# One step of a hybrid decoder layer on one core: h goes into the gate unnormalised, half of its tiles turned by transposing DMAs, and the embedding tiles are loaded later

## The chip, the cores and the metric

The kernel runs on one core of one Trainium2 chip. The metric is the device time of one execution in microseconds (us). The engines are called as the profile calls them: PE is TensorE (matrix products), PEld its weight loads, DVE is VectorE, ACT is ScalarE, POOL is GpSimd, and SP is SyncE, which issues most DMAs. All data is float32; products of float32 accuracy are made from two parts of each operand, a high part in the format fp32r and the low remainder (names that end in h and l).

## What is computed

The layer has a part A (gated mixing), a part B (pooling), an output projection, and last a gated embedding. Only the end of the layer matters here:

```
h = h + _rmsnorm(jnp.einsum('bld,de->ble', m, w_out), post_g)
e = jnp.einsum('blp,pd->bld', p, w_ple)
gate = jax.nn.sigmoid(jnp.einsum('bld,de->ble', _rmsnorm(h, ple_in_g), w_pg))
h = h + _rmsnorm(gate * e, ple_out_g)
```

There are 1024 prompt tokens in eight tiles of 128 (tiles 0 to 7) and 8 sample tokens (tile S); the model is 1024 wide. _rmsnorm(h, g) is h times one root per token times the gain g per column.

## The kernel before

**Products.** Each 1024 x 1024 product is done with Strassen's scheme: seven products of half blocks (P1 to P7) instead of eight, on sums of quarters of both operands. The stored operand has parts B11, B21, B22 and the sums T1 to T4, each loaded and cut into a high and a low part; for wg (the gate's weights w_pg) the parts T4 and B22 lie in DRAM already cut (wgcut, tiles wgT4h, wgT4l, wgB22h, wgB22l). The sums are built in the middle of the kernel by column_sums (line 1340): it loads two row blocks of w_pg (wgraw), cuts parts of them, adds and subtracts them in place on VectorE, and stores the results (wglow, wghigh). column_steps (line 1358) hangs this on steps of part B.

**Stages.** The last stages are the output projection (names wo, m, mw) and the gate (wg, h, hw). Both go over four pairs of token tiles: pair i holds tiles 2i and 2i + 1. In both the tokens are the stationary operand, and each pair's sums of quarters (hs) are cut into hw. A product's result (acct, in PSUM) is taken out by ScalarE or VectorE.

**Between the two stages.** After pair i of the output stage, each of its tiles goes through four functions, hung on the steps of the next pair:
- out_finish (line 1408) scales the row, adds x by an accumulating DMA on POOL's queue, and stores h to DRAM by SP.
- gate_norm (line 1417) takes the mean square of h on ScalarE (hn<-h, whose full output is only scratch), the root on VectorE and POOL (ms, rstd), and scales h into hn on VectorE.
- gate_input (line 1425) turns hn into big, eight blocks of 128 x 128, on TensorE (pht<-ident,hn); ScalarE takes each block out with the gain ple_in_g of its row of w_pg as scale (big<-pht,gvec).
- For the sample, gate_input multiplies the gain in sample_stationary (line 801), which writes sst.

**The embedding.** ge_start (line 1453) allocates the gate's output tile ge and loads the stored embedding e into eback. It is called by Embed.loads (line 1490), that is, with the weights of the pair, FETCH = 6 steps ahead. gated (line 1457) applies the sigmoid, multiplies by eback, takes the mean square and, for tiles 6 and 7 and S, multiplies by the gain row out. gate_finish (line 1471) scales by the root and adds h: for tiles 0 to 5 by an accumulating DMA, for the last two by scalar_tensor_tensor (STT) with a loaded hback, in two halves that are stored apart.

**The order.** All instructions from step 3 on are recorded and then ordered by a planner (class Planner, line 56): TensorE's list is the clock, and every other operation gets a due time from it (late) and is placed on its engine by due time, when the planner takes its operands and a slot of SBUF to be free. So a small change can move instructions of all engines. The helpers record all operations, and the profile therefore shows line 299 for each; groups are told apart by tile names. SP and the queue of each engine run in order.

**The transposing DMA that exists already.** For v, in the first stage, v_planes (line 873) splits the 32-bit words of a tile into two planes of 16 bits (vw<-v, on ScalarE), dma_start_transpose turns them (v<-vw, issued on SP), and v_join (line 882) puts the planes together in big (big<-v, on ScalarE).

Of the kernel before, what the change touches and what calls it, by code (L numbers as in the profile page):

```python
# [8 lines left out]
F32 = mybir.dt.float32  # L9
F32R = mybir.dt.float32r  # L10
BF16 = mybir.dt.bfloat16
U16 = mybir.dt.uint16
AF = mybir.ActivationFunctionType
ALU = mybir.AluOpType

P = 128
D = 1024
NB = D // P
# [3 lines left out]
HALF = 512  # L22
# [283 lines left out]
def hybrid_step(  # L306
# [7 lines left out]
    nc = tc.nc  # L314
# [3 lines left out]
    dram = ctx.enter_context(tc.tile_pool(name="spill", bufs=1, space=bass.MemoryType.DRAM))  # L318
# [6 lines left out]
    w_in, w_pa, w_pb, w_out, w_ple, w_pg = w_in[0], w_pa[0], w_pb[0], w_out[0], w_ple[0], w_pg[0]  # L325
# [4 lines left out]
    def slot(name, shape=(P, T), dt=F32):  # L330
        n_name[0] += 1
        return plan.tile(spool.tile(list(shape), dt, tag="slot", name=f"{name}_{n_name[0]}", bufs=SLOTS,
                                    padded_shape=None), "slot")

    def sm(name):
        n_name[0] += 1
        return small.tile([P, 1], F32, tag="sm", name=f"{name}_{n_name[0]}")
# [17 lines left out]
    def dma(out, in_, by=None):  # L355
        (by or nc.sync).dma_start(out=out, in_=in_)
# [11 lines left out]
    ident = cpool.tile([P, P], F32, tag="ident", name="ident")  # L368
# [6 lines left out]
    nc = plan  # L375
# [3 lines left out]
    big = cpool.tile([P, NB, T], F32, tag="big", name="big")  # L379

    def rstd(parts, n=P):

        t, r = sm("ms"), sm("rstd")
        nc.vector.tensor_scalar(out=t[:n], in0=parts[0][:n], scalar1=EPS,
                                scalar2=parts[1][:n] if len(parts) == 2 else 0.0, op0=ALU.add, op1=ALU.add)
        nc.gpsimd.tensor_tensor(out=r[:n], in0=t[:n], in1=mhalf[:n], op=ALU.pow)
        return r

    def root(part, n=P):

        t, r = sm("ms"), sm("rstd")
        nc.vector.tensor_scalar(out=t[:n], in0=part[:n], scalar1=EPS, scalar2=None, op0=ALU.add)
        nc.gpsimd.tensor_tensor(out=r[:n], in0=t[:n], in1=mhalf[:n], op=ALU.pow)
        return r

    def square_sum(src, n=P, bias=0.0, scratch=None):

        s = sm("ssq")
        out = junk[:n, : src.shape[1]] if scratch is None else scratch[:n]
        nc.scalar.activation(out=out, in_=src, func=AF.Square, scale=D ** -0.5, bias=bias, accum_out=s[:n])  # L400
        return s
# [12 lines left out]
    class Operand:  # L414
# [37 lines left out]
        def at(self, what, k):  # L452
            return [part[:, k % 2, :] for part in self.parts[what, k // 2]]
# [237 lines left out]
    class User:  # L691

        func = AF.Copy
# [5 lines left out]
        def loads(self):  # L699
            pass  # L700
# [100 lines left out]
    def sample_stationary(src, nk, gain=None):  # L801

        st = slot("sst", (P, nk, P), F32R)
        nc.gpsimd.memset(f32(st), 0.0)
        ps = bank("psst").rearrange("p (k t) -> p k t", t=16)
        for k in range(nk):
            nc.tensor.transpose(ps[:, k, :NS], src[:NS, k * P : (k + 1) * P], ident[:NS, :NS])
        got = ps[:, :nk, :NS]
        if gain is not None:
            mul(smix_s, got, gain.unsqueeze(2).to_broadcast([P, NB, NS]))  # L810
            got = smix_s
        split(got, st[:, :, :NS], st[:, :, 32 : 32 + NS])
        return st
# [21 lines left out]
    col = lambda i, k: gvec[:, i * NB + k : i * NB + k + 1]  # L835
# [26 lines left out]
    S = NB  # L862
    rows = lambda t: NS if t == S else P
# [4 lines left out]
    NPAIR = NB // 2  # L868
    vsums = cpool.tile([P, NB + 1, NPAIR], F32, tag="vsums", name="vsums")
# [138 lines left out]
    kept = {}  # L1008
# [4 lines left out]
        kept[key + "high"] = dram.tile([HALF, HALF + w], F32, tag=key + "high", name=key + "high")  # L1013
    wgcut = {what: dram.tile([HALF, D], F32, tag="wg" + what, name="wg" + what) for what in ('T4', 'B22')}
    kept["rowsum"] = dram.tile([NB, P], F32, tag="rowsum", name="rowsum")
    kept["h"] = dram.tile([T, D], F32, tag="h", name="h")
    kept["e"] = dram.tile([T, D], F32, tag="e", name="e")

# [20 lines left out]
    def stored(key, src, width, free=None, split=()):  # L1039
        return Stored(key, src, kept[key + "low"], kept[key + "high"], width, free, split)  # L1040
# [7 lines left out]
    class Gate(User):  # L1048
        func = AF.Sigmoid
# [7 lines left out]
    class U(User):  # L1057
        func = AF.Gelu_apprx_tanh
# [4 lines left out]
    class ZA(User):  # L1063
        func = AF.Silu
# [84 lines left out]
    class ZB(User):  # L1149
        func = AF.Silu  # L1150
# [90 lines left out]
    flat, c = big.rearrange("p b t -> p (b t)"), [T + 4 * w for w in (0, HALF, HALF + WIDE, HALF + 2 * WIDE)]  # L1241
# [20 lines left out]
    c = vsteps[0]  # L1262
# [67 lines left out]
    p, l, c = gbsteps[2], gbsteps[3], pasteps[0]  # L1330
    turn_over(yaop, l, [*l[1:], c[0]])
    p, l, c = pasteps[2], pasteps[3], pbsteps[0]
# [7 lines left out]
    def column_sums(key, src, b):  # L1340

        lo, hi = raw = [slot(f"{key}raw", (P, D)) for _ in range(2)]
        for i, t in enumerate(raw):
            dma(t, src[(4 * i + b) * P : (4 * i + b + 1) * P, :])

        def go():
            cuts = wgcut if key == "wg" else {}
            for what, src in (("B11", lo[:, :HALF]), ("B21", hi[:, :HALF]), ("B22", hi[:, HALF:])):
                if what in cuts:
                    store_parts(cuts[what], b, src)  # L1350
            store_sums(key, b, lo, hi, HALF)
            for what, src in (("T2", lo[:, :HALF]), ("T1", lo[:, HALF:]), ("T4", hi[:, :HALF]), ("T3", hi[:, HALF:])):
                if what in cuts:
                    store_parts(cuts[what], b, src)

        return go

    def column_steps(key, src, steps):
        for b, (l, c) in enumerate(steps):
            held = []  # L1360
            at(l, lambda b=b, held=held: held.append(column_sums(key, src, b)))
            at(c, lambda held=held: held[0]())

    column_steps("wo", w_out, [(uflow[8 + 5 * i], uflow[11 + 5 * i]) for i in range(4)])
    bflow = [s for x, z, _ in bsteps for p in (x, z) for s in p]
    column_steps("wg", w_pg, [(bflow[9 + 7 * i], bflow[12 + 7 * i]) for i in range(4)])

    def sample_product(st, op):

# [6 lines left out]
        return left, right  # L1376

    half = lambda j: slice(j * HALF, (j + 1) * HALF)
    h_of, parts, hn_of, samples = {}, {}, {}, {}

    def start(t, name):
        h_of[t], parts[t] = slot(name, (P, D)), []
# [25 lines left out]
    def out_finish(t):  # L1408
# [5 lines left out]
        nc.gpsimd.dma_start(out=h, in_=x_of(t), accum_op=ALU.add)  # L1414
        dma(kept["h"][t * P : t * P + r, :], h)

    def gate_norm(t):

        r = rows(t)
        h = h_of.pop(t)  # L1420
        hn = hn_of[t] = slot("hn", (P, D))
        rs = rstd([square_sum(h[:r], r, scratch=hn)], r)
        nc.vector.tensor_scalar_mul(hn[:r], h[:r], rs[:r])

    def gate_input(t):

        hn = hn_of.pop(t)
        if t == S:
            samples["h"] = sample_stationary(hn, NB, gvec[:, 2 * NB :])
            return  # L1430
        for k4 in range(0, NB, 4):
            ps = bank("pht")
            for k in range(4):
                nc.tensor.transpose(ps[:, k * P : (k + 1) * P], hn[:, (k4 + k) * P : (k4 + k + 1) * P], ident)
            for k in range(4):
                nc.scalar.activation(out=big[:, k4 + k, t * P : (t + 1) * P], in_=ps[:, k * P : (k + 1) * P],
                                     func=AF.Copy, scale=col(2, k4 + k))

    def merged_sample():
        st = samples["m"] = slot("mst", (P, NB, P), F32R)  # L1440
# [12 lines left out]
    def ge_start(t):  # L1453
        ge[t], e_of[t], parts[t] = slot("ge", (P, D)), slot("eback", (P, D)), []
        dma(e_of[t][: rows(t)], kept["e"][t * P : t * P + rows(t), :])

    def gated(t, c, src):
        r = rows(t)
        g = ge[t][:r, c]
        nc.scalar.activation(out=g, in_=src, func=AF.Sigmoid)  # L1460
        mul(g, e_of[t][:r, c], g)
        parts[t].append(square_sum(g, r))
        if len(parts[t]) > 2:
            a, b = parts[t][:2]
            both = sm("both")
            nc.vector.tensor_scalar(out=both[:r], in0=a[:r], scalar1=b[:r], scalar2=None, op0=ALU.add)
            parts[t][:2] = [both]
        if t >= NB - 2:
            mul(g, g, gains["out"][:r, c])
# [17 lines left out]
            dma(y_of(t)[:, half(j)], g[:r, half(j)])  # L1487

    class Embed(User):
        def loads(self):  # L1490
            for m in range(2):
                ge_start(2 * self.pair + m)

        def direct(self, m, j, ps, c=None):
            gated(2 * self.pair + m, c or half(j), ps)

# [20 lines left out]
    LAST = ("P1", "P6", "P7", "P4", "P5", "P3", "P2")  # L1517

    FIRST = ("P1", "P7", "P6", "P2", "P4", "P5", "P3")
    woop, wgop = stored("wo", w_out, HALF), stored("wg", w_pg, HALF, split=wgcut)  # L1520
    outsteps = [strassen(Turned(i, "m"), woop, Out(i), Tokens, None if i else FIRST) for i in range(NPAIR)]
    gatesteps = [strassen(Turned(i, "h"), wgop, Embed(i), Tokens, LAST if i == NPAIR - 1 else None)
                 for i in range(NPAIR)]
# [5 lines left out]
    l, c = pbsteps[3], outsteps[0]  # L1529
    turn_over(woop, l, [*l[2:], c[0], c[1]], ("B11", "T3", "T2", "B21", "T4", "T1", "B22"))  # L1530
    l, c = outsteps[3], gatesteps[0]
    turn_over(wgop, [s if what not in wgcut else e for what, s, e in zip(PARTS, l, [*l[1:], c[0]])], [*l[2:], c[0], c[1]])

    def gain_row(key, src):
        gains[key] = row_broadcast(src, key)

    at(pbsteps[3][4], lambda: gain_row("post", post_g[0]))
    at(outsteps[3][4], lambda: gain_row("out", ple_out_g[0]))
    at(outsteps[0][1], merged_sample)
    at(outsteps[1][2], out_sample)  # L1540
    at(outsteps[1][4], lambda: out_finish(S))
# [183 lines left out]
```

## Time and profile before

| what | value |
|---|---|
| three runs | 993.88, 996.26, 996.41 us (median 996.26) |
| the profiled execution | 993.25 us |
| its span in the profile | 991.5 us |
| PE busy | 977.7 us |
| DVE busy | 802.9 us |
| ACT busy | 522.8 us |
| POOL busy | 69.6 us |
| last product starts | 983.12 us |
| granted clock of TensorE, mean | 0.997 |

Busy times are those of the engine's instructions without waits. In a timeline row stand start, duration, engine, line, operation, tiles (out<-in), shapes and how many follow one another; in brackets the idle time before it and what ended it. A group's row has the least, median and most duration in ns and the first and last start. A busy PE is not PE at its peak, since products overlap; so the distance between starts is used for it. The span leaves out some 1.7 us that the execution's own time has around it.

### The profile page before, as it was taken

The numbers are of one execution on the slowest core, as the hardware profiler recorded it, in microseconds if no ns is written. First come the engines' busy times: TensorE is split into PE (matmuls) and PEld (weight loads), VectorE is DVE, ScalarE is ACT, GpSimd is POOL, SyncE is SP. The second block draws the span as 40 slices with busy tenths as digits, with TensorE's granted clock in tenths as the row PEclk, the third lists the DMA queues.
The fourth block names the chain that finished last, engine by engine and source line by source line (L and its number), as shares of the span: only waits on it lengthen the run. The fifth ranks groups of instructions, "written<-read, shape, count | busy, mean of one in ns | idle before, by whom it ended". The sixth has DMA issues, their size and how long they took to land. (4 is left out here: it accounts for less than half of the span.)

```text
span 991.5 us, 16004 instructions
## 1 busy us (share of the span) xinstructions
PE 977.7 (99%) x6110; PEld 878.0 (89%) x6110; DVE 802.9 (81%) x1245; ACT 522.8 (53%) x923; POOL 69.6 (7%) x142
## 2 busy tenths in 40 slices
PE   8999999999999999999999999999999999999996
PEld 6899989999998999999999999999999988888885
DVE  5976559787769888888897987697799898779797
ACT  7778887565434433243342333562453365678653
POOL 2000001000000000000000100000000002312111
PEclk9999999999999999999999999999999999999998
DMA  9335573322374354564635076873663553389546
GB/s 336 131 107 113 123 151 128 127 84 76 120 258 146 128 196 141 196 209 155 242 118 192 16 260 214 316 282 126 238 233 131 173 186 85 79 279 360 158 109 191
DMA packets 105515, 171.39 MB, mean 173 GB/s; under 512 B 25375, under 2 KB 65775, under 8 KB 105430
## 3 DMA queue, kind: packets, MB, share of 16 engines
q1 hardware_dynamic: 103070, 162.46, 48.2%
q0 software_dynamic: 2048, 7.37, 4.2%
q8 instruction: 48, 0.79, 0.3%
q10 hardware_dynamic: 320, 0.54, 0.2%
q14 instruction: 29, 0.24, 0.1%
HBM read 114.84 MB, written 51.77 MB: 168 GB/s over the span
## 5 line engine op out<-in xcount | busy, mean ns | idle before, releaser
L299 DVE TENSOR_TENSOR u<-acc,u 128x520 f32<-128x520 f32 (+1 forms) x90 | 62.6, 696 | 36.4 <-PE acc L299 31.9
L299 POOL TENSOR_TENSOR rstd<-ms,mhalf 128x1 f32<-128x1 f32 (+1 forms) x45 | 37.3, 830 | 215.7 <-DVE ms L299 215.7
L299 POOL MEMSET u<- 128x8 f32 x35 | 4.7, 135 | 497.5 <-PE acc L299 270.7
L299 ACT ACTIVATE u<-acc 128x512 f32<-128x512 f32 x39 | 23.2, 595 | 27.5 <-PE acc L299 27.1
L299 ACT ACTIVATE paw<-pas 128x512 fp32r<-128x512 f32 x16 | 10.0, 628 | 30.6 <-DVE pas L299 25.2
L299 ACT ACTIVATE pbw<-pbs 128x512 fp32r<-128x512 f32 x16 | 10.0, 629 | 26.8 <-DVE pbs L299 23.7
L299 DVE TENSOR_TENSOR big<-big 128x1024 f32<-128x1024 f32 (+4 forms) x20 | 23.6, 1217 | 0.0
L299 ACT ACTIVATE big<-pht,gvec 128x128 f32<-128x128 f32 x64 | 18.0, 382 | 8.3 <-PE pht L299 8.3
L299 ACT ACTIVATE big<-mix 128x256 f32<-128x256 f32 x32 | 12.1, 383 | 17.3 <-PE mix L299 16.6
L299 ACT ACTIVATE big<-v 128x1024 uint16<-128x1024 uint16 x16 | 18.5, 1174 | 4.7 <-DMA v<-vw 4.7
L299 PE MATMUL accm<-qh,wpoolw 128*128 128x260 f32 (+1 forms) x96 | 20.9, 319 | 0.0
L299 ACT ACT_TABLE_LOAD x13 | 16.7, 1283 | 6.8 <-PE acc L299 5.8
L299 ACT ACTIVATE gbw<-gbs 128x512 fp32r<-128x512 f32 x16 | 10.0, 625 | 15.6 <-DVE gbs L299 13.7
L299 DVE TENSOR_TENSOR acc<-acc,u 128x512 f32<-128x512 f32 (+1 forms) x16 | 11.2, 699 | 8.7 <-PE acc L299 8.7
L299 ACT ACTIVATE zbw<-zbs 128x512 fp32r<-128x512 f32 x16 | 10.1, 629 | 15.1 <-DVE zbs L299 9.5
L299 ACT ACTIVATE zaw<-zas 128x512 fp32r<-128x512 f32 x16 | 10.0, 630 | 14.6 <-DVE zas L299 9.1
L299 ACT ACTIVATE zbw<-zbraw 128x512 fp32r<-128x512 f32 x12 | 7.5, 626 | 19.2 <-DMA zbraw<-in_w_in_dram 10.5
L299 PEld LDWEIGHTS accm<-qh,wpoolw 128*128 128x128 f32 x96 | 15.6, 188 | 1.9
L299 ACT ACTIVATE uw<-us 128x512 fp32r<-128x512 f32 x16 | 10.0, 626 | 13.6 <-DVE us L299 10.8
L299 DVE TENSOR_TENSOR v<-acc,u 128x520 f32<-128x520 f32 (+1 forms) x9 | 6.3, 697 | 13.4 <-PE acc L299 13.4
L299 ACT ACTIVATE gb<-gb 128x1032 f32<-128x1032 f32 (+1 forms) x8 | 6.8, 854 | 18.7 <-DVE gb L299 18.7
L299 ACT ACTIVATE vw<-v 128x1024 uint16<-128x1024 uint16 x16 | 16.1, 1045 | 0.5 <-DVE v L299 0.5
(688 smaller groups left out, 3626.6 us busy)
## 6 DMA issues: line engine op xcount, KB each, us to landing
ga<-ga SPq DMA_DIRECT2D x16, 516.0 KB
gb<-gb SPq DMA_DIRECT2D x16, 516.0 KB
ya<-za SPq DMA_DIRECT2D x8, 516.0 KB
yb<-zb SPq DMA_DIRECT2D x8, 516.0 KB
x<-in_x_prompt_dram SPq DMA_DIRECT2D x8, 512.0 KB
vraw<-in_w_in_dram SPq DMA_DIRECT2D x8, 512.0 KB
e<-e SPq DMA_DIRECT2D x8, 512.0 KB
garaw<-in_w_in_dram SPq DMA_DIRECT2D x8, 512.0 KB
```

The lines of the kernel that those rows point to most:

```text
L299: getattr(getattr(self.nc, e), method)(*args, **kwargs)
```

## The change

1. **No normalisation ahead of the gate.** gate_norm still takes the mean square and the root, but keeps the root in rin(t), a column of vsums, which is free by then. h goes to the product as it is. gated multiplies by the root: scale=rin(t) in the sigmoid. The scaling of hn on VectorE is gone.
2. **The gain ple_in_g goes into w_pg.** column_sums scales both row blocks by the gain on ScalarE before the sums, and stores their left halves to a new DRAM tile, wgleft (the parts B11 and B21 are loaded from there instead of w_pg). The loads and the sums hang on earlier steps of part B: 7 + 7i and 9 + 7i instead of 9 + 7i and 12 + 7i.
3. **Tiles 0 to 3 are turned by DMA.** gate_norm splits h into two planes of 16 bits (hw<-h, two ScalarE instructions; this hw is another tile than the cut sums of that name) and turns them with a transposing DMA back into h; gate_input joins the planes into big (big<-h, two ScalarE instructions). Tiles 4 to 7 are turned by TensorE as before, with one eviction of 512 columns per four blocks instead of four of 128.
4. **The embedding tiles come later.** ge_start is called at step 5 of the pair before instead of with the weights.

```
-        hn = hn_of[t] = slot("hn", (P, D))
-        rs = rstd([square_sum(h[:r], r, scratch=hn)], r)
-        nc.vector.tensor_scalar_mul(hn[:r], h[:r], rs[:r])
+        nc.scalar.activation(out=spare, in_=src, func=AF.Square, scale=D ** -0.5, accum_out=n[:r])
+        root(n, r, rin(t))
+        if t not in BY_DMA:
+            return
+        words = slot("hw", (P, 2, D), U16)
+        for w in range(2):
+            nc.scalar.activation(out=words[:, w], in_=h.bitcast(U16).rearrange("p (c w) -> p w c", w=2)[:, w],
+                                 func=AF.Copy)
+        h_of[t] = h.bitcast(U16).rearrange("p (k t) -> p k t", t=P)
+        nc.sync.dma_start_transpose(out=h_of[t], in_=words.rearrange("p w c -> p (w c)"))
...
+            if t in BY_DMA:
+                nc.scalar.activation(out=words_of(t)[:, k4].rearrange("p k (t w) -> p k t w", w=2),
+                                     in_=got.rearrange("p (w k) t -> p k t w", w=2)[:, k4], func=AF.Copy)
+                continue
...
-            for k in range(4):
-                nc.scalar.activation(out=big[:, k4 + k, t * P : (t + 1) * P], in_=ps[:, k * P : (k + 1) * P],
-                                     func=AF.Copy, scale=col(2, k4 + k))
+            nc.scalar.activation(out=big[:, k4, t * P : (t + 1) * P], in_=ps.rearrange("p (k t) -> p k t", t=P),
+                                 func=AF.Copy)
...
+            for i, t in enumerate(raw if cuts else ()):
+                nc.scalar.activation(out=t, in_=t, func=AF.Copy, scale=col(2, 4 * i + b))
+                dma(kept["wgleft"][(4 * i + b) * P : (4 * i + b + 1) * P, :], t[:, :HALF])
...
-    column_steps("wg", w_pg, [(bflow[9 + 7 * i], bflow[12 + 7 * i]) for i in range(4)])
+    column_steps("wg", w_pg, [(bflow[7 + 7 * i], bflow[9 + 7 * i]) for i in range(4)])
...
-        nc.scalar.activation(out=g, in_=src, func=AF.Sigmoid)
+        nc.scalar.activation(out=g, in_=src, func=AF.Sigmoid, scale=rin(t))
...
-        def loads(self):
-            for m in range(2):
-                ge_start(2 * self.pair + m)
-
...
+    for i in range(NPAIR):
+        at((gatesteps[i - 1] if i else outsteps[3])[5], lambda i=i: [ge_start(2 * i + m) for m in range(2)])
```

How the instructions move is shown at three places. First TensorE, in the output stage, where pair 1 goes from its step P5 (woT1) to P1 of the next product (woB11); before:

```order
L299 MATMUL acct_1331<-woT1l_1267,mw_1308 128x512
L299 MATMUL acct_1331<-woT1h_1266,mw_1308 128x512
L299 MATMUL pht_1339<-ident,hn_1300 128x128 x4
L299 MATMUL pht_1340<-ident,hn_1300 128x128 x4
L299 MATMUL acct_1344<-woB11h_1221,mw_1322 128x512
```

and now:

```order
L299 MATMUL acct_1330<-woT1h_1267,mw_1307 128x512 x2
L299 MATMUL acct_1330<-woT1l_1268,mw_1307 128x512
L299 MATMUL acct_1330<-woT1h_1267,mw_1307 128x512
L299 MATMUL acct_1338<-woB11h_1222,mw_1321 128x512
L299 MATMUL acct_1338<-woB11l_1223,mw_1321 128x512
```

The eight transposes are gone, and the products follow one another; the same holds at three more places. Second SP, where the weights of the gate's first pair are loaded (wgB from w_pg or wgleft, wgT from the stored sums, h<-h the store of h). Before:

```order
L299 DMA wgB_1257_1386<-in_w_pg_dram 128x2x512
L299 DMA eback_1394<-e 128x1024
L299 DMA eback_1392<-e 128x1024
L299 DMA wgT_1268_1397<-wglow 128x2x512
L299 DMA wgT_1269_1398<-wglow 128x2x512
L299 DMA wgB_1285_1414<-in_w_pg_dram 128x2x512
L299 DMA wgB_1286_1415<-in_w_pg_dram 128x2x512
L299 DMA h<-h_1369 128x1024
L299 DMA wgT_1293_1422<-wghigh 128x2x512
```

and now:

```order
L299 DMA wgB_1244_1374<-wgleft 128x2x512
L299 DMA_TRANSPOSE h_1308<-hw_1351 128x16x128
L299 DMA wgT_1251_1381<-wglow 128x2x512
L299 DMA_TRANSPOSE h_1323<-hw_1348 128x16x128
L299 DMA wgT_1252_1382<-wglow 128x2x512
L299 DMA wgB_1264_1394<-wgleft 128x2x512
L299 DMA wgB_1265_1395<-wgleft 128x2x512
L299 DMA wgT_1272_1402<-wghigh 128x2x512
```

The two loads of eback and the store of h have left this stretch (the first load of eback now stands behind wgT4, and one store of h fewer stands ahead of wgT4's end), and the transposing DMAs of tiles 2 and 3 have come in. Third VectorE, at the very end (ge_1550 and ge_1548 before are ge_1546 and ge_1544 now, tiles 7 and 6). Before:

```order
L299 TENSOR_TENSOR ge_1548<-acct_1582,u_1574 128x512
L299 SCALAR_TENSOR_TENSOR ge_1550<-ge_1550,rstd_1585,hback_1586 128x512
L299 TENSOR_TENSOR ge_1548<-eback_1549,ge_1548 128x512
L299 TENSOR_TENSOR ge_1548<-eback_1549,ge_1548 128x256
L299 SCALAR_TENSOR_TENSOR ge_1550<-ge_1550,rstd_1585,hback_1586 128x512
```

and now:

```order
L299 TENSOR_TENSOR ge_1544<-acct_1562,u_1554 128x512
L299 SCALAR_TENSOR_TENSOR ge_1546<-ge_1546,rstd_1565,hback_1566 128x512 x2
L299 TENSOR_TENSOR ge_1544<-eback_1545,ge_1544 128x512
L299 TENSOR_TENSOR ge_1544<-eback_1545,ge_1544 128x256
L299 TENSOR_SCALAR both_1570<-ssq_1567,ssq_1568 128x1
```

Both halves of tile 7's STT now stand ahead of the products with eback for tile 6.

More of the change, by code (lines that the diff above doesn't have):

```diff
@@ L387, in rstd, with root @@
         return r
-    def root(part, n=P):
-        t, r = sm("ms"), sm("rstd")
+    def root(part, n=P, r=None):
+        t, r = sm("ms"), sm("rstd") if r is None else r
         nc.vector.tensor_scalar(out=t[:n], in0=part[:n], scalar1=EPS, scalar2=None, op0=ALU.add)
@@ L1015, in hybrid_step @@
     kept["rowsum"] = dram.tile([NB, P], F32, tag="rowsum", name="rowsum")
+    kept["wgleft"] = dram.tile([D, HALF], F32, tag="wgleft", name="wgleft")
     kept["h"] = dram.tile([T, D], F32, tag="h", name="h")
@@ L1378, in hybrid_step @@
     half = lambda j: slice(j * HALF, (j + 1) * HALF)
-    h_of, parts, hn_of, samples = {}, {}, {}, {}
+    h_of, parts, samples = {}, {}, {}
     def start(t, name):
@@ L1415, in out_finish, with words_of @@
         dma(kept["h"][t * P : t * P + r, :], h)
+    rin = lambda t: vsums[: rows(t), t, :1]
+    BY_DMA = (0, 1, 2, 3)
+    def words_of(t):
+        return big.bitcast(U16)[:, :, 2 * t * P : 2 * (t + 1) * P]
     def gate_norm(t):
         r = rows(t)
-        h = h_of.pop(t)
-        hn = hn_of[t] = slot("hn", (P, D))
-        rs = rstd([square_sum(h[:r], r, scratch=hn)], r)
-        nc.vector.tensor_scalar_mul(hn[:r], h[:r], rs[:r])
+        h = h_of[t]
+        n, spare = sm("ssq"), slot("hspare", (P, D))[:r] if t == S else big[:, :, t * P : (t + 1) * P]
+        src = h[:r] if t == S else h.rearrange("p (k c) -> p k c", c=P)
+        nc.scalar.activation(out=spare, in_=src, func=AF.Square, scale=D ** -0.5, accum_out=n[:r])
[8 more added lines that the diff above has]
+        nc.sync.dma_start_transpose(out=h_of[t], in_=words.rearrange("p w c -> p (w c)"))
@@ L1425, in gate_input @@
     def gate_input(t):
-        hn = hn_of.pop(t)
+        got = h_of.pop(t)
         if t == S:
-            samples["h"] = sample_stationary(hn, NB, gvec[:, 2 * NB :])
+            samples["h"] = sample_stationary(got, NB)
             return
-        for k4 in range(0, NB, 4):
+        for k4 in (slice(0, 4), slice(4, NB)):
+            if t in BY_DMA:
+                nc.scalar.activation(out=words_of(t)[:, k4].rearrange("p k (t w) -> p k t w", w=2),
+                                     in_=got.rearrange("p (w k) t -> p k t w", w=2)[:, k4], func=AF.Copy)
+                continue
@@ L1432, in gate_input @@
             ps = bank("pht")
             for k in range(4):
-                nc.tensor.transpose(ps[:, k * P : (k + 1) * P], hn[:, (k4 + k) * P : (k4 + k + 1) * P], ident)
-            for k in range(4):
-                nc.scalar.activation(out=big[:, k4 + k, t * P : (t + 1) * P], in_=ps[:, k * P : (k + 1) * P],
-                                     func=AF.Copy, scale=col(2, k4 + k))
+                nc.tensor.transpose(ps[:, k * P : (k + 1) * P], got[:, (k4.start + k) * P : (k4.start + k + 1) * P], ident)
@@ L1519, in hybrid_step @@
     FIRST = ("P1", "P7", "P6", "P2", "P4", "P5", "P3")
-    woop, wgop = stored("wo", w_out, HALF), stored("wg", w_pg, HALF, split=wgcut)
+    woop, wgop = stored("wo", w_out, HALF), stored("wg", kept["wgleft"], HALF, split=wgcut)
     outsteps = [strassen(Turned(i, "m"), woop, Out(i), Tokens, None if i else FIRST) for i in range(NPAIR)]
```

## The prediction

> **What bounds the kernel now.** I read the page first, for the shares of the engines, then the waits of TensorE, then the timeline of TensorE around the removed work. From the page:
>
> ```profile
> PE 977.7 (99%) x6110; PEld 878.0 (89%) x6110; DVE 802.9 (81%) x1245; ACT 522.8 (53%) x923; POOL 69.6 (7%) x142
> ```
>
> The reader is to see PE at 977.7 of 991.5 us. The waits of TensorE are seven rows in all, of which these are the first and the last (total, times, longest):
>
> ```profile
> PE warm L299 <- POOL ident masks.py:199: 1.9, 1, 1.9
> ...
> PE state L299 <- DVE big L299: 0.3, 1, 0.3
> ```
>
> The seven sum to 5.7 us and none lies in the output or gate stage. So TensorE sets the end: whatever is taken from its list comes off the time in full, if nobody else becomes late; and work on another engine costs nothing as long as TensorE finds its operands and its PSUM tiles ready.
>
> **What the change removes.** Half of the pht transposes leave TensorE. This is one tile of them in TensorE's timeline before (start, duration, operation):
>
> ```profile
> 848.19 0.40 PE L299 MATMUL acct<-woT1h,mw 128*128 128x512 f32 x1
> 848.43 1.03 PE L299 MATMUL pht<-ident,hn 128*128 128x128 f32 x8
> 849.22 0.48 PE L299 MATMUL acct<-woB11h,mw 128*128 128x512 f32 x1
> 849.54 0.39 PE L299 MATMUL acct<-woB11l,mw 128*128 128x512 f32 x1
> ```
>
> Durations overlap in the pipeline, so starts count. From the first transpose to the next product is 849.22 − 848.43 = 0.79 us; that product is followed after 0.32 us, where the usual step (848.19 to 848.43) is 0.24. The eight transposes so cost 0.79 + 0.08 ≈ 0.88 us, a quarter of what the summed durations would say. Four tiles: 4 × 0.88 = **−3.5 us**. Tiles 4 to 7 stay on TensorE.
>
> VectorE loses the scaling of hn, and ScalarE changes its evictions. Their groups, from the views of the tiles hn and pht (ns: least, median, most), and from the page the two operations that the DMA path uses, as the kernel already does it for v:
>
> ```profile
> L299 DVE TENSOR_SCALAR hn<-h,rstd x8: 732/748/752, 841.0 to 923.9; 128x1024 f32<-128x1024 f32 x8
> L299 ACT ACTIVATE big<-pht,gvec x64: 347/378/415, 849.1 to 927.3; 128x128 f32<-128x128 f32 x64
> L299 ACT ACTIVATE big<-v 128x1024 uint16<-128x1024 uint16 x16 | 18.5, 1174 | 4.7 <-DMA v<-vw 4.7
> L299 ACT ACTIVATE vw<-v 128x1024 uint16<-128x1024 uint16 x16 | 16.1, 1045 | 0.5 <-DVE v L299 0.5
> ```
>
> VectorE: −8 × 0.748 = −6.0 us, off the path, but it is slack where it is full. ScalarE on a DMA tile: two splits and two joins, 2 × 1.045 + 2 × 1.174 = 4.4 us, for eight evictions, 8 × 0.378 = 3.0 summed: +1.4 us, and up to +2.2 since evictions in a row overlap, four times. On a TensorE tile two evictions of 512 columns, about the 0.6 us of u<-acc (595 ns in the page's groups) each, replace eight: about −1 us, four times. ScalarE is the engine with room, so I take nothing for this:
>
> ```profile
> 843.00:873.00 30.00, 30.00 (x149) 24.60 (x148) 23.60 (x43) 21.36 (x58) 9.03 (x11) 1.00 0.34 84
> 873.00:893.00 20.00, 20.00 (x97) 16.45 (x96) 15.28 (x21) 14.04 (x32) 3.44 (x5) 1.00 1.04 331
> 893.00:913.00 20.00, 20.00 (x93) 16.33 (x92) 18.05 (x26) 15.39 (x36) 5.34 (x5) 1.00 1.05 357
> ```
>
> These windows (span; PE, PEld, DVE, ACT, POOL busy; clock; DMA share; GB/s) show ScalarE busy 70 to 77%. They also show what matters more, the last two columns: the DMA engines are two thirds idle until 873 and **full from 873 to 913**.
>
> **What the transposing DMAs cost.** The v stage has eight; two with their joins, from the queues of SP and ScalarE, and what the DMA engines did from 75 to 85 us (40 slices of 0.25 us):
>
> ```profile
> 75.45 1.99 SPq L299 DMA_TRANSPOSE v<-vw  x1
> 79.08 1.77 SPq L299 DMA_TRANSPOSE v<-vw  x1
> ```
>
> ```profile
> 79.85 1.19 ACT L299 ACTIVATE big<-v 128x1024 uint16<-128x1024 uint16 x1 [1.18 <-DMA v<-vw]
> 83.42 1.19 ACT L299 ACTIVATE big<-v 128x1024 uint16<-128x1024 uint16 x1 [0.78 <-DMA v<-vw]
> ```
>
> ```profile
> DMA  0000000999999999922008999999999699899940
> GB/s 0 0 0 0 0 0 5 184 221 213 202 221 217 218 215 196 193 37 41 0 0 162 217 206 218 214 215 222 216 182 217 159 266 233 299 336 348 315 135 21
> ```
>
> A join waited until 4.4 us after the issue (75.45 to 79.85), and 4.3 the second time. Ten full slices, 2.5 us of all sixteen engines, went into one tile at some 215 GB/s. Tiles 0 and 1 turn near 850 to 860, in idle DMA time: free. For one of tiles 2 and 3 the evictions of pht began here before:
>
> ```profile
> 870.98 2.18 ACT L299 ACTIVATE big<-pht,gvec 128x128 f32<-128x128 f32 x8 [0.20 <-PE pht L299]
> ```
>
> In the new order their splits and transposing DMAs stand some instructions behind that place, near 875 to 880, in the full stage: +5.0 us of DMA work ahead of the gate's weights.
>
> [...] The slices above say 215 GB/s, so I go by 2.5.
>
> **Who is late then.** The last loads that TensorE needs early in the gate are the two halves of wgT4. Their issues on SP, and those eight DMAs later (the order has each issue wait for the eighth before it):
>
> ```profile
> 887.71 0.51 SPq L299 DMA_DIRECT2D wgT4h<-wgT  x1
> ...
> 891.29 0.39 SPq L299 DMA_DIRECT2D wgT4h<-wgT  x1
> 892.60 0.36 SPq L299 DMA_DIRECT2D wgT4l<-wgT  x1
> ...
> 899.07 0.36 SPq L299 DMA_DIRECT2D wgB22h<-wgB  x1
> 900.37 0.36 SPq L299 DMA_DIRECT2D wgB22l<-wgB  x1
> 901.96 1.30 SPq L299 DMA_DIRECT2D eback<-e  x2
> ```
>
> The first wgT4h has landed by 899.1, its wgT4l by 900.4, a store of h by 902.0; in steps of about 1.3 us the second pair follows by 902.9 and 904.2 (an estimate from these rows). TensorE reads the second pair here (the second product of the first row is the first on the second half):
>
> ```profile
> 908.35 0.63 PE L299 MATMUL acct<-wgT4h,hw 128*128 128x512 f32 x2
> 908.81 0.39 PE L299 MATMUL acct<-wgT4l,hw 128*128 128x512 f32 x1
> ```
>
> So before there were 908.81 − 904.2 = 4.6 us to spare. The change takes 3.5 of them by TensorE coming earlier. On the DMA side it adds 5.0 us and takes three 512 KB transfers out from ahead of wgT4's end (two eback loads and one store of h, 1.3 us each by the same steps): net +1.1. To that comes up to 1.4 us in which SP stands before a transposing DMA until ScalarE has split its tile, with the queue empty (nothing is left where eback stood). New landing 905.3 to 906.7, wanted at 905.3: a wait of 0 to 1.4 us. Bounds: if transposes ran at the plain rate, no wait; if both slowed plain loads beside them by as much again, 5 us. I take the nearest rows and the low middle, **+0.5 us**. wgB22 has 3 us more to spare (first read at 915.55) and is covered.
>
> **The tail.** The end runs through VectorE, ScalarE and POOL after the last product:
>
> ```profile
> 982.61 0.74 DVE L299 SCALAR_TENSOR_TENSOR ge<-ge,rstd,hback 128x512 f32<-128x512 f32 x1
> 983.40 1.03 DVE L299 TENSOR_TENSOR ge<-eback,ge 128x512 f32<-128x512 f32 x2
> 985.20 0.42 ACT L299 ACTIVATE junk<-ge 128x256 bf16<-128x256 f32 x1 [0.36 <-issue]
> 986.73 1.42 DVE L299 SCALAR_TENSOR_TENSOR ge<-ge,rstd,hback 128x512 f32<-128x512 f32 x2 [0.44 <-POOL rstd L299]
> ```
>
> In the new order both halves of the first STT stand ahead of the eback products; two such take 1.42 us (row 986.73) where one takes 0.74. The products start 0.65 to 0.7 later, and junk, rstd and the last STT with them: **+0.65 us**. The new scale of the sigmoid is hidden under that STT; its price is between nothing and 0.1 us.
>
> **The early part of the change.** Eight scalings of wgraw on ScalarE, eight stores of wgleft and earlier loads lie between 410 and 530 us. A 128x1024 pass of ScalarE took 1.05 us for vw, above. Two windows of the stretch:
>
> ```profile
> 460.00:480.00 20.00, 20.00 (x130) 18.23 (x130) 19.56 (x32) 9.17 (x15) 0.66 (x3) 1.00 0.42 148
> 500.00:520.00 20.00, 20.00 (x135) 18.40 (x135) 19.90 (x31) 8.73 (x14) 1.78 (x5) 1.00 0.27 93
> ```
>
> That is 8.4 us of ScalarE in 120, where it is busy 46%, and DMA time at a share of 0.27 to 0.42: covered, 0. The uncovered part is VectorE, 98% busy: its in-place sums of wgraw now also wait for the wgleft store to have read the tile, with the adds that free TensorE's PSUM queued behind them. No row shows that wait; it is between 0 (the store was issued long before) and the 4 us of a landing above. I take 0, since the steps also start earlier, and keep the other end as a rival.
>
> **Sum**, against the profiled execution's 993.25 us: −3.5 + 0.5 + 0.65 = −2.35, so 990.9. The median of the runs shown is 996.26, 3.0 above that execution; on it the forecast is **993.9**.
>
> **The rivals.**
> 1. *wgT4 is in time* and the tail costs little: −2.85 to −3.5, about 993.1. For it: the slices count a whole tile at 2.5 us though the loads could fill gaps between its packets. Against it: a share of 1.04 from 873 on. [...]
> 2. *VectorE waits for wgleft* between 410 and 530: one or two waits of 2 to 4 us, less a cover that I put at 1 to 2 us: +1.5 on the forecast, 995.4. For it: 19.90 of 20 us busy. Against: DMA is two thirds idle there.
> 3. *Slower: the transposed tiles land late.* A DMA in the full stage lands 11.4 us after its issue (887.71 to 899.07), and with transposes among those ahead up to 13.8; not 4.4. ScalarE meets the first join of tile 2 some 3.5 us after the issue (the instructions between them in the new order) and stands in order, with wgB11h, wgT2h, the hw pieces and the evictions of acct behind it, for 8 to 10 us. The hw pieces bound it: before, the last was ready 3.1 us ahead of the first gate product:
>
> ```profile
> 888.57 0.62 ACT L299 ACTIVATE hw<-big 128x512 fp32r<-128x512 f32 x1
> ```
>
> ```profile
> L299 PE MATMUL acct<-wgB11h,hw x32: 388/396/477, 892.3 to 963.5; 128*128 128x512 f32 x32
> ```
>
> So TensorE would wait 5 to 7 us, wgT4's wait being hidden in it: −2.85 + 6 = +3.15, 999.4. TensorE waits from a landing of 6.6 us on, and the kernel is slower than before from 9.5 us on. For it: the DMA share. Against it: SP stands before this DMA, so little is queued ahead of it. [...]
> 4. *Nothing gained*: TensorE reaches the gate early and waits there for VectorE, which is 18.05 of 20 us busy from 893 to 913. Against: VectorE loses 6.0 us just there. About 996.3.
>
> **How the numbers follow.** Chances: forecast 0.33, rivals 0.28, 0.17, 0.19, 0.03. The bound of 0.3%, about what a measurement of this kernel can tell from no change, is 3.0 us. Faster by more: 0.21 of the first rival and 0.09 of the forecast, 0.30. Slower by more: 0.13 of the third and 0.06 of the second, whose upper end is two waits of 4 us, 0.19. The rest, 0.51, is within. The three runs before spread over 2.5 us, so the low end is the first rival's −3.5 less 1.6: 991.2. The high end is the third's 999.4.
>
> **What would show it.** Right: four pht rows left for 32 matmuls, TensorE's busy time 3.5 us down, at most one new wait of TensorE, on wgT4, under 1.5 us, and a tail of about 9 us from the last product. Wrong: a ScalarE wait for the DMA of h above 5 us, a VectorE wait between 410 and 530, or several TensorE waits on acct or hw in the gate.

## The result and the profile after

The change made the kernel slower: 1011.8 us median of 6 runs (1009.36 to 1016.78) against 996.25 us of 6 runs of the kernel before, ratio 1.0161 with a 95% interval of 1.0142 to 1.018. The forecast was 993.9 us in a range up to 999.4.

Page of the changed kernel, its span and busy times:

```profile
span 1010.7 us, 15931 instructions
...
PE 983.5 (97%) x6078; PEld 879.9 (87%) x6078; DVE 797.8 (79%) x1235; ACT 536.1 (53%) x891; POOL 67.6 (7%) x142
```

VectorE has lost 5.1 us of work and ScalarE gained 13.3, about as worked out. TensorE is busy 5.8 us longer, though 32 matmuls are gone, and no longer 99% of the span. What it waited for from 850 us on (total, times, longest):

```profile
PE acct L299 <- ACT h L299: 6.0, 1, 6.0
PE acct L299 <- DVE h L299: 2.0, 1, 2.0
PE acct L299 <- DMA wgB22l<-wgB: 1.8, 2, 0.9
PE pht L299 <- ACT big L299: 0.8, 1, 0.8
PE acct L299 <- DMA wgB22h<-wgB: 0.6, 1, 0.6
```

Before, there was none of these. I set each matmul of the changed kernel beside the same one of before and followed the difference of their starts. It is +5.2 us before the first removed transposes, falls by 0.85 to 0.88 at each of the four places (to +1.8 at 879 us: the saving is there in full), and then rises to +18.9 at the last matmul. The 5.2 us ahead of the gate are not of the change: TensorE's list is the same up to there, and most of the loss sits at the start (1.6 us) and near 150 us (about 3.1), in instructions that the change does not touch. From 321 to 849 us the difference stays at 5.2, so the work that the change adds between 410 and 530 us cost nothing that shows here.

So the gate lost 17.1 us. ScalarE's queue first, in the first of these views, then SP's and POOL's:

```profile
882.87 0.62 ACT L299 ACTIVATE hw<-big 128x512 fp32r<-128x512 f32 x1
894.30 1.17 ACT L299 ACTIVATE big<-h 128x1024 uint16<-128x1024 uint16 x1 [10.81 <-DMA h<-hw]
895.38 0.57 ACT L299 ACTIVATE junk<-acct 128x512 bf16<-128x512 f32 x1
895.86 0.19 ACT L299 ACTIVATION_READ_ACCUMULATOR junk<-acct 128x1 f32 x1
895.95 0.58 ACT L299 ACTIVATE h<-acct 128x512 f32<-128x512 f32 x1
```

```profile
876.24 1.26 SPq L299 DMA_DIRECT2D wgB<-wgleft  x2
880.48 4.30 SPq L299 DMA_TRANSPOSE h<-hw  x1
884.88 1.02 SPq L299 DMA_DIRECT2D wgT<-wglow  x1
886.00 11.88 SPq L299 DMA_TRANSPOSE h<-hw  x1
897.97 0.53 SPq L299 DMA_DIRECT2D wgT<-wglow  x1
```

```profile
880.44 0.90 POOL L299 DMA_DIRECT2D h<-in_x_prompt_dram  x1 [2.00 <-PE acct L299]
886.04 0.87 POOL L299 DMA_DIRECT2D h<-in_x_prompt_dram  x1 [3.12 <-DVE h L299]
```

The reader is to see three things. The join of tile 2 stood 10.81 us for a transposing DMA that was issued at 880.48 and landed by 894.30: 13.8 us. The eviction h<-acct, for which TensorE waited 6.0 us, stood behind it. And the issue of the second transposing DMA held SP for 11.88 us, with the gate's weights behind it: the second wgT of the first sum was issued only at 897.97. POOL issued an accumulating load of x at the very time of each transpose, and these loads came late too. From the DMA view, the two loads before (issued at 876.65 and 881.50) and now (the last column: us from issue to landing):

```profile
h<-in_x_prompt_dram POOLq DMA_DIRECT2D x1, 512.0 KB, 8.4
h<-in_x_prompt_dram POOLq DMA_DIRECT2D x1, 512.0 KB, 8.6
```

```profile
h<-in_x_prompt_dram POOLq DMA_DIRECT2D x1, 512.0 KB, 13.1
h<-in_x_prompt_dram POOLq DMA_DIRECT2D x1, 512.0 KB, 18.8
```

So the collision has three victims in this trace: ScalarE's joins, SP's list, and the accumulating loads themselves. What the DMA engines and TensorE's clock did meanwhile (some of the windows; the last three columns: clock, DMA share, GB/s):

```profile
879.00:882.00 3.00, 3.00 (x15) 2.45 (x14) 1.96 (x3) 3.00 (x6) 0.90 (x1) 1.00 0.90 314
882.00:885.00 3.00, 3.00 (x15) 2.43 (x14) 2.91 (x4) 1.49 (x3) 0.56 (x1) 1.00 1.28 113
888.00:891.00 3.00, 2.62 (x12) 1.77 (x10) 0.56 (x1) 0.00 (x0) 0.00 (x0) 1.00 1.06 79
891.00:894.00 3.00, 0.00 (x0) 0.00 (x0) 0.00 (x0) 0.00 (x0) 0.00 (x0) 1.00 1.27 109
894.00:906.00 12.00, 9.41 (x34) 7.56 (x35) 5.00 (x7) 6.72 (x11) 0.93 (x1) 0.72 1.23 146
897.00:900.00 3.00, 3.00 (x8) 2.32 (x8) 2.39 (x4) 3.00 (x6) 0.93 (x1) 0.50 1.34 135
```

From 882 to 894 the engines are counted as busy all the time (a share of 1.06 to 1.28) and move 79 to 113 GB/s, where a transpose alone moved some 215 (in this kernel too, from 853 to 855 us) and the plain loads and stores of before 395, from 894 to 906 us. And after TensorE had stood for 6.0 us, its granted clock was 0.72 in the mean of 12 us, with 0.50 from 897 to 900. By the starts of its matmuls that cost another 2.5 us: the difference from before rises from 7.8 us at 896.6 to 10.4 at 902.0. A later window, 920 to 930, has 0.88, behind the wait of 2.0 us.

### The profile page after: what moved, and what is told of

Read it like the earlier page. It is cut to its first block, busy times and chain, and to the rows that moved or that the text cites. A ratio compares the mean times of both kernels' runs of the same rounds, so it can differ in the third digit from the quotient of the medians.

```text
span 1010.7 us, 15931 instructions
## 1 busy us (share of the span) xinstructions
PE 983.5 (97%) x6078; PEld 879.9 (87%) x6078; DVE 797.8 (79%) x1235; ACT 536.1 (53%) x891; POOL 67.6 (7%) x142
## 5 line engine op out<-in xcount | busy, mean ns | idle before, releaser
L299 POOL TENSOR_TENSOR rstd<-ms,mhalf 128x1 f32<-128x1 f32 (+1 forms) x36 | 28.4, 790 | 196.8 <-DVE ms L299 196.6
L299 ACT ACTIVATE big<-h 128x1024 f32<-128x1024 f32 (+1 forms) x16 | 17.5, 1115 | 12.5 <-DMA h<-hw 10.8
L299 PE MATMUL acct<-woT1h,mw 128*128 128x512 f32 x32 | 12.6, 457 | 6.0 <-ACT h L299 6.0
L299 PEld LDWEIGHTS accm<-qh,wpoolw 128*128 128x128 f32 x96 | 15.6, 188 | 1.9
L299 ACT ACTIVATE uw<-us 128x512 fp32r<-128x512 f32 x16 | 10.0, 626 | 13.1 <-DVE us L299 11.0
L299 DVE TENSOR_TENSOR v<-acc,u 128x520 f32<-128x520 f32 (+1 forms) x9 | 6.3, 697 | 13.3 <-PE acc L299 13.3
```

Source lines behind the costliest of these rows:

```text
L299: getattr(getattr(self.nc, e), method)(*args, **kwargs)
```

## The experiments

Theory A: the transposes of tiles 2 and 3 collapsed because accumulating loads ran beside them; ScalarE and SP stood in order for them, and TensorE behind both. Rival B: the plain loads of the full stage did it. Rival C: another part of the change did it.

**No tile by DMA.**

```
-    BY_DMA = (0, 1, 2, 3)
+    BY_DMA = ()
```

> No tile of h is turned by DMA: all eight by TensorE, the rest of the change stays. Theory A (the two transposing DMAs of tiles 2 and 3 run 13.8 us and more because POOL's accumulating loads of x are in flight beside them; ScalarE stands 10.8 us at the join, SP 11.9 us at the next issue, and TensorE waits for both): the gate is as before, 32 transposes are back on TensorE (+3.5 us against the change) and the tail is 0.65 us longer, so within 0.2% of before. Rival C (the gain in w_pg, the stores of wgleft or the later embedding loads do the harm): still over 1.0% slower.

Measured: ratio 1.0006 (0.9989 to 1.0023). Rival C falls: the gain in w_pg, the stores of wgleft, the unnormalised h and the later embedding loads together cost nothing that can be measured, in either direction. Its one new row of TensorE in the gate:

```profile
PE acct L299 <- DVE ge L299: 0.3, 1, 0.3
```

**Tiles 0 and 1 alone by DMA.**

```
-    BY_DMA = (0, 1, 2, 3)
+    BY_DMA = (0, 1)
```

> Only tiles 0 and 1 are turned by DMA, in the idle stretch near 850 to 860 us. Theory A: two transposes of 2.5 us each, no ScalarE wait over 2 us at their joins; TensorE gains 2 x 0.87 = 1.75 us and loses 0.65 in the tail: about 1.1 us (0.1%) faster than before, between -0.3% and +0.1%. Rival B (any transposing DMA of h costs ScalarE and SP too much): over 0.5% slower.

Measured: 0.9989 (0.9976 to 1.0002), and once more, in more rounds:

> The run with tiles 0 and 1 by DMA once more, in more rounds, beside the one with three tiles: 0.1% faster than before (0.0 to 0.2%).

0.9997 (0.9983 to 1.001). So between a tenth of a per cent slower and a quarter faster: rival B in its broad form, that any transposing DMA of h costs too much, falls. The two transposes and the load beside the second one, from SP's queue and POOL's:

```profile
849.07 1.81 SPq L299 DMA_TRANSPOSE h<-hw  x1
856.29 5.18 SPq L299 DMA_TRANSPOSE h<-hw  x1
```

```profile
855.57 0.93 POOL L299 DMA_DIRECT2D h<-in_x_prompt_dram  x1 [2.06 <-DMA h<-hs]
```

The second issue lasted 5.18 us, with an accumulating load issued 0.7 us ahead of it (5.17 in the second run, at the same distance). In the DMA records no packet of the transpose starts until that load is nearly through, near 860; then it moves up to 290 GB/s. ScalarE came later than that, so nobody waited.

**The same without that load.** In out_finish, for tiles 2 and 3 (and in the next runs for 4 and 5):

```
-        nc.gpsimd.dma_start(out=h, in_=x_of(t), accum_op=ALU.add)
+        if t in (2, 3):
+            xt = slot("xback", (P, D))
+            nc.sync.dma_start(out=xt, in_=x_of(t))
+            add(h, h, xt)
+        else:
+            nc.gpsimd.dma_start(out=h, in_=x_of(t), accum_op=ALU.add)
```

> Tiles 0 and 1 by DMA, and x of tiles 2 and 3 by plain loads on SP with an add on VectorE, so that no accumulating load runs beside the transpose of the second tile (there its issue lasted 5.18 us on SP beside one, 1.81 alone). Theory A: both issues last about 1.8 us. Nobody waited there, so the time is that of the run with two tiles by DMA within 0.15%, 0 to 0.2% faster than before. If the long issue has another cause, it stays near 5 us.

```profile
850.12 1.77 SPq L299 DMA_TRANSPOSE h<-hw  x1
857.35 1.86 SPq L299 DMA_TRANSPOSE h<-hw  x1
```

Both issues are short now, as theory A says. The time was 1.0008 (0.9995 to 1.002): not the gain that was expected, though the interval overlaps those of the two runs above. In its profiled execution, which was 3.6 us longer than its median, TensorE has a wait of 2.6 us for VectorE (ge) in the gate, where the other run has 0.3; the two adds may be the cause, but that was not tried apart.

**Four tiles, plain loads of x for tiles 4 and 5 on SP.** The decisive one: the edit above with t in (4, 5), on the changed kernel.

> As the change, but x for tiles 4 and 5 comes by a plain load on SP and is added on VectorE (+1.2 us of VectorE each), so that no accumulating DMA of POOL's queue runs beside the transposes of tiles 2 and 3. Theory A: each of the two transposes lands within 6 us of its issue, ScalarE stands less than 3 us at the first join, and the kernel is within 0.5% of before. Rival B (the plain loads of SP's own queue slow the transposes): landings still over 9 us, ScalarE still stands over 6 us, over 1.0% slower.

Measured: 1.0027 (1.0012 to 1.0042), against 1.0161 of the change. SP's queue and ScalarE's:

```profile
877.43 3.02 SPq L299 DMA_TRANSPOSE h<-hw  x1
880.55 0.53 SPq L299 DMA_DIRECT2D xback<-in_x_prompt_dram  x1
881.17 0.38 SPq L299 DMA_DIRECT2D wgT<-wglow  x1
881.65 4.36 SPq L299 DMA_TRANSPOSE h<-hw  x1
```

```profile
882.42 1.19 ACT L299 ACTIVATE big<-h 128x1024 uint16<-128x1024 uint16 x1 [1.14 <-DMA h<-hw]
```

The first transpose landed within 5.0 us of its issue, with plain loads of SP's queue ahead of it and behind, and ScalarE stood 1.14 us. So rival B, in the form recorded here, falls. Five sixths of the loss (0.0134 of 0.0161) are gone with two accumulating loads. What remains in the trace is a wait for weights:

```profile
PE acct L299 <- DMA wgB22l<-wgB: 3.2, 2, 2.4
```

**Joins later in ScalarE's list.** The change, with another number for the planner:

```
-                op.busy, op.moved, op.lands = 3.0, 0.01, 1.5
+                op.busy, op.moved, op.lands = 3.0, 0.01, (1.5 if op.fixed or op.at < 600 else 12.0)
```

> As the change, but the planner is told that a transposing DMA of h lands 12 us after its issue instead of 1.5, so it puts the joins later in ScalarE's list; the transposes still run beside the accumulating loads. If ScalarE's stand at the join is the main cost, its wait of 10.8 us and TensorE's of 6.0 us shrink to under 2 us each and the kernel is 0.2 to 0.8% slower than before. If SP's stand (weights behind the second transpose) is the main cost, it stays over 1.0% slower.

Measured: 1.017 (1.0149 to 1.0192), no better. ScalarE does not stand for a transposing DMA any more, so the time went elsewhere: the planner's number reordered the lists of all engines, TensorE's too, and the program then stands for other things. TensorE's longest waits, and the SP issue of the second transpose:

```profile
PE acct L299 <- ACT hw L299: 4.8, 1, 4.8
PE pht L299 <- DMA h<-in_x_prompt_dram: 3.0, 1, 3.0
PE pht L299 <- ACT big L299: 1.9, 1, 1.9
```

```profile
886.55 8.02 SPq L299 DMA_TRANSPOSE h<-hw  x1
```

The transposes were issued at other times here (874.17 and 886.55), and the two accumulating loads (issued at 881.92 and 885.34) landed in 8.6 and 8.4 us, as before the change: the packets of the second transpose start only when both are through, at 894.0. SP still stood 8.02 us, as the second branch of the expectation has it. But this is another program with losses of its own, and it doesn't tell whether ScalarE's stand or SP's makes the loss of the change; that question stays open. It does show that a later place for the joins, by this number, is no remedy.

**Is it the other queue, or the accumulating?** Two runs with x for tiles 4 and 5 as plain loads on other queues (nc.gpsimd and nc.scalar for nc.sync in the edit above):

> As the change, but x for tiles 4 and 5 comes by plain loads that do not accumulate, on POOL's queue as before, with the add on VectorE. If any traffic of another queue slows a transpose, the landings stay over 9 us and the kernel over 1% slower. If it is the accumulating that does it (packets of 327 ns and more), the landings fall to about 5 us and the kernel is within 0.5% of before.

> As the change, but x for tiles 4 and 5 comes by plain loads on ScalarE's DMA queue, with the add on VectorE. If any traffic of another queue slows a transpose, landings stay over 9 us and the kernel over 1% slower; if only POOL's queue or accumulating does, landings are about 5 us and it is within 0.5% of before.

Measured: 1.0046 (1.0025 to 1.0067) and 1.0018 (1.0002 to 1.0033). Not the collapse; but the runs did not test what they were meant to, since a plain load need not wait for h and was issued earlier (873 to 875 on POOL, 872 to 874 on ScalarE), mostly ahead of the transposes. So a third, in which VectorE first copies a column of h into the target:

```
+            nc.vector.tensor_copy(xt[:, :1], h[:, :1])
             nc.gpsimd.dma_start(out=xt, in_=x_of(t))
```

> As the run with plain loads of x for tiles 4 and 5 on POOL's queue, but the load is made to wait for h (VectorE copies one column of h into its target first), so that it is issued when the accumulating load was, beside the transposes of tiles 2 and 3. If any traffic of another queue slows a transpose, the first lands over 9 us after its issue and the kernel is over 1% slower. If only accumulating loads do, it lands within 7 us and the kernel is 0.2 to 0.8% slower (wgB22 late, as in the other runs with four tiles).

Measured: 1.0034 (1.0016 to 1.0053). SP's queue, POOL's and ScalarE's:

```profile
873.83 4.16 SPq L299 DMA_TRANSPOSE h<-hw  x1
878.71 3.34 SPq L299 DMA_TRANSPOSE h<-hw  x1
```

```profile
873.67 0.60 POOL L299 DMA_DIRECT2D xback<-in_x_prompt_dram  x1 [1.89 <-DVE xback L299]
880.06 0.58 POOL L299 DMA_DIRECT2D xback<-in_x_prompt_dram  x1 [3.78 <-DVE xback L299]
```

```profile
880.07 1.19 ACT L299 ACTIVATE big<-h 128x1024 uint16<-128x1024 uint16 x1 [3.22 <-DMA h<-hw]
```

Issued 0.16 us apart, nearly as in the change (0.04), a plain load of POOL's queue let the first transpose land in 6.2 us instead of 13.8. The second pair was 1.35 us apart, with the load behind, and did not collapse either. So the same queue and the same bytes, issued at about the same distance, do no such harm without accumulating. It is not quite the same test: in the DMA records the packets of the first load end at 877.7, and those of its transpose begin at 877.2; those of the second load begin at 883.3, and its transpose's end at 883.6. The two thus overlap for half a microsecond at most in each pair. What a plain load would do that runs through the whole of a transpose was not tried, so it is not shown that the accumulating itself is the cause. A 4 KB packet of an accumulating load lasts 327 ns as a rule and up to 3.0 us in the collision (up to 1.7 for the same two loads before the change); one of a plain load lasts 159 as a rule.

**The late wgB22.** With four tiles and plain loads TensorE still waited 2 to 3 us for wgB22. First, one embedding load out of its way, on the run with plain loads:

```
-    at((gatesteps[i - 1] if i else outsteps[3])[5], ...
+    at((gatesteps[i - 1] if i else outsteps[3])[6], ...
```

> As the run with plain loads of x for tiles 4 and 5, but the embedding tiles are loaded one step later still, which takes one 512 KB load (eback) from ahead of half of wgB22. If TensorE's wait of 3.2 us for wgB22 there came from the sum of transfers ahead of it, it shrinks by about 1.3 us or more and the kernel is 1 to 3 us faster than that run (within 0.2% of before). If it came from something else, it stays.

Measured: 1.0037 (1.0024 to 1.005), and the wait is 3.2 us as before: a miss. SP's queue shows why. One of the two loads of eback did go behind wgB22, but the planner put another load of 512 KB ahead in its place, that of the gain row out (issued at 899.31; at 906.93, behind wgB22, in the run with plain loads). So as many bytes stand ahead of wgB22 as without the edit, and the run tells nothing of the cause. Then one transpose fewer, on the run with ScalarE's queue:

```
-    BY_DMA = (0, 1, 2, 3)
+    BY_DMA = (0, 1, 2)
```

> Tiles 0, 1 and 2 by DMA, tile 3 by TensorE, and x of tiles 4 and 5 by plain early loads on ScalarE's DMA queue. Theory A with the sum of transfers: one transpose of 2.5 us fewer stands ahead of wgB22 than with four tiles, whose wait there was 2.1 us, so TensorE waits under 0.5 us for it, keeps 3 x 0.87 = 2.6 us and loses 0.3 in the tail: 0.1 to 0.3% faster than before. If wgB22 is late for another reason, its wait stays at 2 us and the kernel is within 0.1% of before.

Measured: **0.9973 (0.9957 to 0.9989)**, 991.67 us: faster than both kernels. TensorE has no wait in the gate. With four tiles on ScalarE's queue it had these, and none of them is left; behind them, the transpose of tile 2 on SP in the run with three tiles:

```profile
PE acct L299 <- DMA wgB22h<-wgB: 1.2, 1, 1.2
PE acct L299 <- DMA wgB22l<-wgB: 0.9, 1, 0.9
```

```profile
876.34 1.96 SPq L299 DMA_TRANSPOSE h<-hw  x1
```

That fits a sum of transfers in the full stage, as the prediction had it for wgT4. It does not show it, since the edit moved more than one transfer: SP issues the first wgB of the gate at 868.74 instead of 871.78, ahead of the transpose, and puts the two loads of eback between the halves of wgB22.

## Why the prediction was wrong

The forecast said −2.35 us in the profiled execution and the sign was wrong. By its own steps:

- *The removed transposes*, 4 × 0.88 = 3.5 us: right. The starts of TensorE's matmuls come 0.85 to 0.88 us closer at each of the four places. (Eight durations of 0.272 us sum to 2.2 us, so this is two fifths of them, not a quarter.)
- *VectorE and ScalarE*: right, and of no weight. The part between 410 and 530 us cost nothing: without DMA tiles the ratio is 1.0006, and in the changed kernel the difference stays level there, so rival 2 was not the case. Rival 4 is answered by the run with three tiles alone, which gained and had no wait for VectorE in the gate.
- *The tail*, +0.65: the last STT starts 4.68 us after the last matmul instead of 4.29, and the span ends 8.68 instead of 8.40 after it: +0.3 to +0.4. The order had moved as read. The products with eback start 0.83 us after the last matmul instead of 0.28, so 0.55 later, and some of that is made up behind them.
- *Transposing DMAs at 2.5 us of the DMA engines, added to the other transfers*: **this step failed.** It priced a transpose from one that ran alone, and let the work of several queues add up by time. Beside an accumulating load the first transpose took 13.8 us from issue to landing (about 12 us of them for packets that take 2 to 3 us in the runs without the collision), the loads 13.1 and 18.8 us instead of 8.4 and 8.6, and the second transpose held SP for 11.9 us. The step "I take the nearest rows" chose the rate of an idle stretch for a place where POOL's accumulating loads run; before, those loads were issued there too, and I listed only SP's transfers.
- *A wait of 0.5 us at wgT4*: no wait at wgT4 came, with the collision or without it. Without it TensorE waited 2 to 3 us at wgB22, behind wgT4, which I had called covered by 3 us. A sum of transfers would give that, but no run shows it apart. SP stood 3.0 us ahead of the first of these transposing DMAs (877.50 to 880.48), not up to 1.4.
- *Rival 3*, the transposed tile lands late, had the course of events with a chance of 0.19: a landing of up to 13.8 us (measured 13.8), ScalarE standing 8 to 10 us (10.8) and TensorE 5 to 7 (6.0). That the landings agree is luck: the 13.8 was counted from transfers ahead in SP's queue, and with plain loads there, but no accumulating load beside it, the transpose landed in 5.0. Its reason against, that SP stands before this DMA and little is queued ahead, was true and beside the point: what slowed it was not ahead of it but beside it, on POOL's queue. And its price, 999.4, left out three costs that came with it: TensorE's other waits (5.2 us together, of which 2.4 for wgB22 on SP's list), the lower clock after the waits (by the starts, 2.5 us behind the first and about 1.5 near 920), and the accumulating loads' own delay, whose share in these waits was not measured apart. The waits and the clock make some 15 of the 17.1 us; the rest is not assigned.

The median moved by 15.6 us. In the two profiled spans it is 19.2, of which 5.2 lie ahead of the gate, in work that is the same in both; 14.0 are the gate and the tail: −3.4, +17.1 and +0.3.

## What to carry to other kernels

Price a DMA where it will run, with every queue that is busy there in the list, POOL's too; the time measured in an idle stretch, 4.4 us from issue to join, was 13.8 us beside an accumulating load. Where an engine that works in order waits for a DMA, price what stands behind it on that engine and on the issuing queue (here ScalarE stood 10.81 us and SP 11.88), and the slower clock that followed TensorE's stand here (0.72 over 12 us). A part of a change that pays in an idle stretch and costs in a full one can be split: three of four tiles, with the loads that collided replaced, gave 0.27% where all four lost 1.6%.

## What the runs showed of the hardware

In the changed kernel a transposing DMA and an accumulating load that were issued together (0.04 us apart) slowed each other out of proportion: 79 to 113 GB/s for all that moved from 882 to 894 us, at a DMA share of 1.06 to 1.28, against some 215 GB/s for the transpose alone, and 12.1 and 10.2 us for the packets of the two transposes, against 2.6 for those of tiles 0 and 1 in the same kernel. The loads landed in 13.1 and 18.8 us instead of 8.4 and 8.6. When the accumulating load was issued 0.7 us ahead (three runs) or 1.2 us (the run with later joins), the transpose's packets waited until the load was nearly through and then took 2.1 to 2.6 us.

In the v stage a pair of transposes is slow in all six kernels read there, also in the one before, with no other load in flight. SP's rows of it, before and in the changed kernel, and the ScalarE row at whose start the rate falls:

```profile
133.79 6.44 SPq L299 DMA_TRANSPOSE v<-vw  x2
```

```profile
136.76 1.28 ACT L299 ACT_TABLE_LOAD   x1
```

```profile
135.11 8.45 SPq L299 DMA_TRANSPOSE v<-vw  x2
```

```profile
138.08 1.28 ACT L299 ACT_TABLE_LOAD   x1
```

The other pairs of issues took 4.5 us. In the four kernels whose packets I followed there, the rate fell within 0.3 us of the start of a table load (before, from 206 GB/s between 135.25 and 136.75 us to 34 between 137 and 139, and in the changed kernel from 215 between 136.5 and 138 to 29 between 138.25 and 143); the pair took 5.4 to 8.5 us in different runs of the same instructions, and TensorE waited 0 to 2.4 us for it. That is of the size of the spread between runs of the kernel before (993.88 to 996.41 us). Whether the table load is the cause was not tried. It has no part in the collision of the gate: the last table load of the changed kernel is at 575.44. What the two slow cases share, if anything, is open. The row at 133.79 stood in the trace of before, and would have told that a transpose does not always run at its own rate.
